# The first modulation of a macaron block: two of eight slices summed by VectorE and ScalarE instead of by small matmuls

## Chip, cores and metric

The kernel runs on one core of a Trainium2 chip, as one program in one launch. The metric is the device time of an execution in microseconds. The profile comes from one execution that the hardware profiler recorded; its engines are called PE (TensorE's matmuls), PEld (TensorE's weight loads), DVE (VectorE), ACT (ScalarE), POOL (GpSimd) and SP (SyncE, which issues the transfers).

## What is computed

One residual block over 512 tokens of width 1024, in float32: a SwiGLU feed-forward half step, a token mixer (gated DeltaNet heads beside latent attention) and a second feed-forward half step. Each of the three reads its input through an adaptive norm, whose shift, scale and gate come from a linear map of a conditioning vector:

```
sc = silu(c)                                  # c: (1, 1024)
mod = sc @ w_ada + b_ada                      # w_ada: (1024, 9 * 1024)
sh1, s1, g1, sh2, s2, g2, sh3, s3, g3 = split(mod, 9)
h = rms(x) * (1 + s1) + sh1                   # x: (512, 1024)
x = x + 0.5 * g1 * swiglu(h, ffn1_w_in, ffn1_w_out)   # d_ff = 2816
x = x + g2 * mixer(rms(x) * (1 + s2) + sh2)
x = x + 0.5 * g3 * swiglu(rms(x) * (1 + s3) + sh3, ffn2_w_in, ffn2_w_out)
```

The change concerns the first modulation alone, that is `sh1` and `s1`: 2 x 1024 numbers, each a sum over the 1024 entries of `sc`.

## The kernel before

The state is kept transposed: eight tiles `xT[kt]` of 128 features x 512 tokens. Every product is made in three passes, since both factors are split into a high part in fp32r and a low remainder (`hh`, `hl` for the activations, `wh`, `wl` for the weights); `mm3` (lines 445 to 449) is one such product of a 128x128 tile of weights with 512 columns.

`phase0` is the first stage. It transposes x, takes the norm, makes the first modulation, and already computes the first six tiles of the feed-forward's first product (three of the gate, three of the other half) into six banks of accumulators `pu`. It goes over the eight slices `kt` of 128 features. For each slice three things are loaded by `phase0_load` (512 KB, 512 KB and 384 KB): the 1024 x 128 pieces of `w_ada` for the shift and for the scale into one tile `ar` of 128 x 8 x 2 x 128 (three buffers), and the 128 x 768 weights of the six tiles into `wr` (four buffers). Loads of two slices are issued ahead of the loop, and step kt issues that of slice kt + 2.

The sum over the 1024 entries of `sc` has eight parts of 128. `phase0_cols` (line 589) makes it on TensorE: for each part the column of `sc`, spread to 32 columns, is the stationary side and 256 columns of `ar` are streamed; the parts go two by two to four groups of 32 columns of the array, so that four partial sums stand in four groups of partitions of an accumulator `pg`. Line 596 is that matmul (sixteen instructions a slice in the trace), and line 599 copies the result to `sg` on ScalarE. `columns` (line 512) then turns the row into two columns with two matmuls: `sg` is stationary, and `sel4`, a column with a one in each of the four groups, adds the four partial sums (line 515). VectorE adds the bias (lines 516 and 517).

In step kt of the loop, the modulation of slice kt + 1 is made while slice kt is multiplied: at the head of the step the sixteen matmuls of slice kt + 1 and (from kt = 1 on) the split of its weights, `wh` on ScalarE (line 217) and `wl` on VectorE (line 218); after two of the six tiles the columns, and then `modulate`: `hm` on VectorE (line 639), `hh` on ScalarE (line 641), `hl` on VectorE (line 633). In step 0 the order of products is another one (lines 555, 571, 572), and the split of slice 1's weights comes behind its modulation.

The whole stage is written inside `in_order` (line 143): its instructions stay in the written order on each engine, SyncE's queue too. Outside such blocks a planner decides, when the program is built, where an instruction goes on its engine; it may put an instruction without such an order between two that have one. Behind the stage, `ada_rest` (line 736) sums the rest of the modulation on VectorE in a like manner (lines 762 and 764, a scaled addition over 512 columns), from tiles that take the memory that `ar` leaves, and `plain` goes on with the feed-forward's other tiles.

Of the kernel before, what the change touches and what calls it, by code (L numbers as in the profile page):

```python
# [15 lines left out]
AF = mybir.ActivationFunctionType  # L16
ALU = mybir.AluOpType
AX = mybir.AxisListType

P = 128  # L20
NT = 512
D = 1024
KT = D // P
# [4 lines left out]
HALF = NT // 2  # L28
KPARTS = ((0, 8), (8, 8), (16, 6))
SEVEN = range(9, 19), range(5, 19)  # L30


def drain(*gens):
# [56 lines left out]
class Block:  # L90
# [51 lines left out]
    @contextmanager  # L142
    def in_order(self, ends=None):

        with self.traced() as block:
            yield
        self.ends = dict(ends or {})
        for i in block:
            if i.engine in self.ends:
                self.follow(i, self.ends[i.engine])  # L150
            self.ends[i.engine] = i.name
# [249 lines left out]
    def plan_units(self):  # L401
# [14 lines left out]

        ffn(ins["ffn1_w_in"][0], ins["ffn1_w_out"][0], 3, range(KT), SEVEN[0])
        w = ins["w_in"][0]
# [58 lines left out]
    def phase0(self):  # L477

        nc = self.nc
        xall = self.const([P, KT, NT], s="xT")  # L480
        self.xT = [xall[:, t, :] for t in range(KT)]
        ss = self.const([P, 2 * NB], s="ss")
        loads = [self.phase0_load(0), self.phase0_load(1)]
        pv = self.aux()
        nc.tensor.transpose(pv[:, :80], self.vecs[:80, :], self.ident[:80, :80])
        self.sc = self.const([P, 8], s="sc")
        nc.scalar.activation(self.sc, pv[:, 72:80], AF.Silu)
        self.vT = self.const([P, 72], s="vT")
        nc.vector.tensor_copy(self.vT, pv[:, :72])
        self.sel4 = self.const([P, 1], s="sel4")  # L490
        nc.vector.tensor_reduce(out=self.sel4, in_=self.ident[:, 0:P:32], axis=AX.X, op=ALU.add)

        def raw(b, j):
            pt = self.aux()
            for t in range(4):
                nc.tensor.transpose(pt[:, t * P:(t + 1) * P], self.xtok[b][j][:, t * P:(t + 1) * P], self.ident)
            nc.vector.tensor_copy(xall[:, 4 * j:4 * j + 4, b * P:(b + 1) * P], pt.rearrange("p (t c) -> p t c", t=4))

        tiles = [(b, j) for b in range(NB) for j in range(2)]
        for b, j in tiles:  # L500
            nc.scalar.activation(self.slot(s="jk"), self.xtok[b][j], AF.Square, accum_out=ss[:, 2 * b + j:2 * b + j + 1])
        for i in (2, 0, 1, 3):
            raw(*tiles[i])
        v = self.small(NB, "v")
        nc.vector.tensor_reduce(out=v, in_=ss.rearrange("p (b j) -> p b j", j=2), axis=AX.X, op=ALU.add)
        r = self.rms_cols(v, NB, D)
        for i in (4, 5, 6):
            raw(*tiles[i])
        self.c1, self.c2 = self.const([P, KT], s="sh"), self.const([P, KT], s="s1")
        self.new_h()  # L510

        def columns(kt, sg, pg):
            k = slice(kt, kt + 1)
            for m in range(2):
                nc.tensor.matmul(pg[:, 256 + m:257 + m], sg[:, m * P:m * P + P], self.sel4, start=True, stop=True)
            nc.vector.tensor_tensor(out=self.c1[:, k], in0=pg[:, 256:257], in1=self.vT[:, k], op=ALU.add)
            nc.vector.scalar_tensor_tensor(out=self.c2[:, k], in0=pg[:, 257:258], scalar=1.0, in1=self.vT[:, 8 + kt:9 + kt],
                                           op0=ALU.add, op1=ALU.add)

        def weights(kt):  # L520
            raw, hi, lo = loads[kt][1]
            self.split_w(raw[:, :6, :], hi[:, :6, :], lo[:, :6, :])
            return hi, lo


        xn = self.slot(s="xn")
        for b in range(NB):
            nc.vector.tensor_scalar(out=xn[:, b * P:(b + 1) * P], in0=self.xtok[b][0][:, :P], scalar1=r[:, b:b + 1],
                                    scalar2=None, op0=ALU.mult)
        dg = self.diag(r)  # L530
        cols = self.phase0_cols(0, loads[0][0])
        raw0, wh, wl = (x[:, :6, :] for x in loads[0][1])
        w = wh, wl
        nc.scalar.copy(wh, raw0)
        pt = self.aux()
        for b in range(NB):
            nc.tensor.transpose(pt[:, b * P:(b + 1) * P], xn[:, b * P:(b + 1) * P], self.ident)
        t, m = self.slot(s="hm"), self.slot(s="hm")
        nc.vector.tensor_copy(t, pt)
        columns(0, *cols)  # L540
        hh, hl = self.h[0]
        nc.scalar.activation(hh, t, AF.Identity, scale=self.c2[:, 0:1], bias=self.c1[:, 0:1])
        nc.vector.tensor_scalar(out=m, in0=t, scalar1=self.c2[:, 0:1], scalar2=self.c1[:, 0:1], op0=ALU.mult, op1=ALU.add)
        nc.vector.tensor_tensor(out=hl, in0=m, in1=hh.bitcast(F32), op=ALU.subtract)
        nc.vector.tensor_tensor(out=wl, in0=raw0, in1=wh.bitcast(F32), op=ALU.subtract)
        raw(*tiles[7])
        pu = [self.acc() for _ in range(3)] + [self.aux() for _ in range(3)]
        for kt in range(KT):
            (hi, lo), (xh, xl) = w, self.h[kt]
            more = kt + 1 < KT  # L550
            if kt + 2 < KT:
                loads.append(self.phase0_load(kt + 2))
            if kt == 0:
                for j in range(6):
                    nc.tensor.matmul(pu[j], hi[:, j, :], xh, start=True, stop=False)
                rb = self.slot(s="rb")
                nc.scalar.copy(rb, self.spread_diag(dg, NB))
            for j in range(6):
                if j == 0 and more:
                    cols = self.phase0_cols(kt + 1, loads[kt + 1][0])  # L560
                    if kt > 0:
                        w = weights(kt + 1)
                if j == 2 and more:
                    columns(kt + 1, *cols)
                    self.modulate([kt + 1], slice(0, NT), rb, self.c2, self.c1)
                    if kt == 0:
                        w = weights(kt + 1)
                if kt > 0:
                    self.mm3(pu[j], hi[:, j, :], lo[:, j, :], xh, xl, False, kt == KT - 1)
                else:  # L570
                    nc.tensor.matmul(pu[j], hi[:, j, :], xl, start=False, stop=False)
                    nc.tensor.matmul(pu[j], lo[:, j, :], xh, start=False, stop=False)
        return pu
# [15 lines left out]
    def phase0_cols(self, kt, a):  # L589

        nc = self.nc
        pg = self.aux()
        for q in range(4):
            for e in range(2):
                kc = 2 * q + e
                nc.tensor.matmul(pg[32 * q:32 * q + 32, :256], self.sc[:, kc:kc + 1].to_broadcast([P, 32]),  # L596
                                 a[:, kc], start=(e == 0), stop=(e == 1), tile_position=(0, 32 * q))
        sg = self.slot(s="sg")[:, :256]
        nc.scalar.copy(sg, pg[:, :256])
        return sg, pg  # L600


    def new_h(self):
# [1510 lines left out]
```

## Time and profile before

| what | us |
|---|---|
| median of 3 runs | 1058.62 (1057.68 to 1059.16) |
| profiled execution, its own time | 1057.94 |
| its span, first to last instruction | 1056.2 |
| busy: PE / PEld / DVE / ACT / POOL | 1035.7 / 904.3 / 722.5 / 471.2 / 25.2 |
| mean granted clock of TensorE | 0.997 |

Times in the profile are counted from the start of the span. A matmul's recorded end is modelled, and consecutive matmuls overlap in the records; the chain of work that ended last gives each the time that it adds. A row of the timeline has the start, the duration, the engine, the line, the operation with its output and inputs, the count, and in brackets the idle time of the engine before it and what ended that. A row of the groups has line, engine, operation, names and shapes, the count, then busy us and the mean ns of one. A row of the waits has who waited for whom, the sum of us, how often, and the longest.

### The profile page before, as it was taken

How to read it: one execution, taken by the hardware profiler on the slowest of the kernel's cores; microseconds unless marked ns; L12 is line 12 of the kernel's file. 1: busy time of each engine (PE TensorE's matmuls, PEld its weight loads, DVE VectorE, ACT ScalarE, POOL GpSimd, SP SyncE). 2: the span in 40 equal slices, each digit the busy share in tenths (PEclk: the TensorE clock that was granted, in tenths of full speed). 3: DMA queues.
4: the chain of work that ended last, by engine and by line, in shares of the span. 5: the costliest groups of instructions: out<-in, count | busy, mean ns of one | idle time of the engine just before them, and what ended most of it. 6: DMA issues, size and time to landing. Idle time of an engine off the chain costs nothing.

```text
span 1056.2 us, 16319 instructions
## 1 busy us (share of the span) xinstructions
PE 1035.7 (98%) x6417; PEld 904.3 (86%) x6417; DVE 722.5 (68%) x1280; ACT 471.2 (45%) x857; POOL 25.2 (2%) x74
## 2 busy tenths in 40 slices
PE   6999999999999999999999989999999999999998
PEld 5788799998887798888788769998999999778887
DVE  4479978769888547558787477788688886842221
ACT  3342345555222225469864554354455556422221
POOL 0000000000100000100000001100000000000000
PEclk8999999999999999999999999999999999999999
DMA  9988234343789435211232021113333344723320
GB/s 276 285 260 278 82 100 119 102 121 91 256 287 339 130 96 158 78 40 41 61 80 66 21 80 41 40 42 99 98 103 101 102 119 141 227 76 111 112 62 30
DMA packets 208028, 130.74 MB, mean 124 GB/s; under 512 B 13890, under 2 KB 192079, under 8 KB 207951
## 3 DMA queue, kind: packets, MB, share of 16 engines
q1 hardware_dynamic: 207950, 129.69, 41.3%
q8 instruction: 50, 0.82, 0.3%
q14 instruction: 28, 0.22, 0.1%
HBM read 127.18 MB, written 2.49 MB: 123 GB/s over the span
## 4 chain that ended last, share of the span: by engine, by line
PE 89%; DVE 5%; ACT 2%; DMA 2%; issue 2%; SPq 0%; POOL 0%; DVEq 0%; POOLq 0%; ACTq 0%
PE pa L447 18%; PE pa L448 18%; PE pa L449 18%; PE pa L335 13%; PE pb L335 10%; PE pb L447 1%; PE pb L448 1%; PE pb L449 1%; PE pb L596 1%; PE pb L1847 1%; DVE wl L218 1%; PE pb L1827 1%; DMA xt<-in_x 0%; DVE cv L1391 0%; ACT bd L1477 0%
## 5 line engine op out<-in xcount | busy, mean ns | idle before, releaser
L217 ACT CAST wh<-wr 128x1024 fp32r<-128x1024 f32 (+1 forms) x116 | 116.4, 1008 | 245.8 <-PE pa L448 216.7
L218 DVE TENSOR_TENSOR wl<-wr,wh 128x1024 fp32r<-128x1024 f32 (+1 forms) x116 | 135.3, 1169 | 117.5 <-ACT wh L217 113.3
L447 PE MATMUL pa<-hh,wh 128*128 128x512 f32 (+1 forms) x453 | 174.8, 386 | 1.6 <-ACT sg L808 1.6
L448 PE MATMUL pa<-hl,wh 128*128 128x512 f32 (+1 forms) x453 | 172.8, 381 | 0.0
L449 PE MATMUL pa<-hh,wl 128*128 128x512 f32 (+1 forms) x453 | 172.7, 381 | 0.0
L447 PE MATMUL pa<-ah,wh 128*128 128x512 f32 (+1 forms) x396 | 146.6, 370 | 0.0
L449 PE MATMUL pa<-ah,wl 128*128 128x512 f32 (+1 forms) x396 | 144.9, 366 | 0.0
L448 PE MATMUL pa<-al,wh 128*128 128x512 f32 (+1 forms) x396 | 144.8, 366 | 0.0
L447 PEld LDWEIGHTS pa<-hh,wh 128*128 128x128 f32 x453 | 85.3, 188 | 20.7 <-ACT sg L808 3.0
L449 PEld LDWEIGHTS pa<-hh,wl 128*128 128x128 f32 x453 | 85.3, 188 | 15.8 <-DVE wl L218 0.4
L448 PEld LDWEIGHTS pa<-hl,wh 128*128 128x128 f32 x453 | 85.4, 188 | 14.3 <-DVE hl L633 0.2
L447 PEld LDWEIGHTS pa<-ah,wh 128*128 128x128 f32 x396 | 74.7, 189 | 14.3 <-ACT wh L217 1.7
L449 PEld LDWEIGHTS pa<-ah,wl 128*128 128x128 f32 x396 | 74.7, 189 | 12.3
L448 PEld LDWEIGHTS pa<-al,wh 128*128 128x128 f32 x396 | 74.7, 189 | 11.8
L764 DVE SCALAR_TENSOR_TENSOR aa<-ar,sc,aa 128x512 f32<-128x512 f32 x98 | 73.0, 749 | 9.3 <-DMA ar<-in_w_ada 7.7
L252 DVE TENSOR_TENSOR wl<-sf,wh 128x1024 fp32r<-128x1024 f32 x48 | 58.6, 1222 | 30.0 <-ACT wh L256 30.0
L335 PE MATMUL pa<-hh,wh 128*128 128x256 f32 x192 | 54.5, 284 | 0.0
L335 PE MATMUL pa<-th,wh 128*128 128x256 f32 x192 | 54.3, 283 | 0.0
L335 PE MATMUL pa<-tl,wh 128*128 128x256 f32 x192 | 54.3, 283 | 0.0
L335 PE MATMUL pa<-th,wl 128*128 128x256 f32 x192 | 54.3, 283 | 0.0
L335 PE MATMUL pa<-hl,wh 128*128 128x256 f32 x192 | 54.3, 283 | 0.0
L335 PE MATMUL pa<-hh,wl 128*128 128x256 f32 x192 | 54.3, 283 | 0.0
(434 smaller groups left out, 2214.1 us busy)
## 6 DMA issues: line engine op xcount, KB each, us to landing
wr<-in_ffn_w_in SPq DMA_DIRECT2D x79, 512.0 KB, 3.8
ar<-in_w_ada SPq DMA_DIRECT2D x80, 256.0 KB, 5.9
ar<-in_w_ada SPq DMA_DIRECT2D x32, 512.0 KB, 7.6
wr<-in_ffn_w_out SPq DMA_DIRECT2D x32, 512.0 KB, 3.9
wr<-in_w_in SPq DMA_DIRECT2D x21, 512.0 KB, 3.7
wr<-in_ffn_w_out SPq DMA_DIRECT2D x16, 384.0 KB, 3.6
wr<-in_w_out SPq DMA_DIRECT2D x8, 512.0 KB
wr<-in_ffn_w_in SPq DMA_DIRECT2D x8, 384.0 KB, 7.0
```

Of the source, the lines that this page charges most:

```text
L217: self.nc.scalar.copy(hi, raw)
L218: self.nc.vector.tensor_tensor(out=lo, in0=raw, in1=hi.bitcast(F32), op=ALU.subtract)
L252: sub = lambda out, x, y: nc.vector.tensor_tensor(out=out, in0=x, in1=y, op=ALU.subtract)
L335: nc.tensor.matmul(z, a[:, j, :], b, start=start and j == 0 and i == 0, stop=j == 3 and i == 2, skip_group_check=not start)
L447: mm(out, wh, xh, start=start, stop=False)
L448: mm(out, wh, xl, start=False, stop=False)
L449: mm(out, wl, xh, start=False, stop=stop)
L596: nc.tensor.matmul(pg[32 * q:32 * q + 32, :256], self.sc[:, kc:kc + 1].to_broadcast([P, 32]), a[:, kc], start=(e == 0), stop=(e == 1), til ...
L764: nc.vector.scalar_tensor_tensor(out=acc, in0=a, scalar=sc, in1=acc, op0=ALU.mult, op1=ALU.add)
L1827: nc.tensor.matmul(ps[:, :n], self.qnT[h][:, ts], self.knT[h][:, :n], start=True, stop=False)
L1847: nc.tensor.matmul(po[:, :P], pT[:, b * P:(b + 1) * P], v[b][:, h * P:(h + 1) * P], start=(b == 0), stop=(b == i))
```

## The change

Slices 5 and 7 (`SUMMED`) no longer go through the sixteen small matmuls. `phase0_sums` makes their sum per partition: ScalarE multiplies the first of the eight parts by its entry of `sc` (128 x 256), and seven scaled additions of VectorE add the others, each onto the result of the one before. The partition sum that is left is made by the two column matmuls, with a column of ones instead of `sel4`. The sum for slice kt + 2 is written at the head of step kt, and its instructions are left out of the order written by hand (`loose`), so that the planner places them. For these two slices the columns stand at the head of the step before any product; for the others they now stand after one tile instead of two. The loads of three slices are issued ahead of the loop, and step kt issues that of slice kt + 3.

```diff
+SUMMED = (5, 7)
 ...
     def in_order(self, ends=None):
+        self.loose = set()
         with self.traced() as block:
             yield
         self.ends = dict(ends or {})
         for i in block:
+            if i.name in self.loose:
+                continue
             if i.engine in self.ends:
                 self.follow(i, self.ends[i.engine])
             self.ends[i.engine] = i.name
 ...
-        loads = [self.phase0_load(0), self.phase0_load(1)]
+        loads = [self.phase0_load(kt) for kt in range(3)]
 ...
-        def columns(kt, sg, pg):
+        def columns(kt, sg, pg, ones):
             k = slice(kt, kt + 1)
             for m in range(2):
-                nc.tensor.matmul(pg[:, 256 + m:257 + m], sg[:, m * P:m * P + P], self.sel4, start=True, stop=True)
+                nc.tensor.matmul(pg[:, 256 + m:257 + m], sg[:, m * P:m * P + P], ones, start=True, stop=True)
 ...
+        sums = {}
         for kt in range(KT):
             (hi, lo), (xh, xl) = w, self.h[kt]
             more = kt + 1 < KT
-            if kt + 2 < KT:
-                loads.append(self.phase0_load(kt + 2))
+            if kt + 3 < KT:
+                loads.append(self.phase0_load(kt + 3))
 ...
             for j in range(6):
+                if j == 0 and kt + 2 in SUMMED:
+                    sums[kt + 2] = self.phase0_sums(loads[kt + 2][0])
                 if j == 0 and more:
-                    cols = self.phase0_cols(kt + 1, loads[kt + 1][0])
+                    if kt + 1 in SUMMED:
+                        cols = sums[kt + 1], self.aux(), self.ones[:, 0:1]
+                    else:
+                        cols = self.phase0_cols(kt + 1, loads[kt + 1][0])
                     if kt > 0:
                         w = weights(kt + 1)
-                if j == 2 and more:
+                if j == (kt + 1 not in SUMMED) and more:
                     columns(kt + 1, *cols)
 ...
-        return sg, pg
+        return sg, pg, self.sel4
+
+    def phase0_sums(self, a):
+        nc = self.nc
+        sg = self.slot(s="sg")[:, :256]
+        with self.traced() as block:
+            nc.scalar.activation(sg, a[:, 0], AF.Copy, scale=self.sc[:, 0:1])
+            for kc in range(1, KT):
+                nc.vector.scalar_tensor_tensor(out=sg, in0=a[:, kc], scalar=self.sc[:, kc:kc + 1], in1=sg, op0=ALU.mult,
+                                               op1=ALU.add)
+        self.loose.update(i.name for i in block)
+        return sg
```

## The prediction

> **What bounds the kernel now.** I read the page first, then the chain that ended last, cut to the stage that the change touches, then the timeline of VectorE and ScalarE there, and last the transfers.
>
> ```profile
> PE 1035.7 (98%) x6417; PEld 904.3 (86%) x6417; DVE 722.5 (68%) x1280; ACT 471.2 (45%) x857; POOL 25.2 (2%) x74
> 33.23:39.02 5.79, 5.79 (x40) 4.23 (x39) 2.59 (x5) 1.83 (x3) 0.00 (x0) 1.00 1.11 305
> 39.02:44.80 5.78, 5.78 (x40) 4.22 (x39) 2.60 (x5) 1.83 (x3) 0.00 (x0) 1.00 1.14 310
> 50.58:56.36 5.78, 5.78 (x40) 4.22 (x39) 2.63 (x6) 1.83 (x3) 0.00 (x0) 1.00 0.46 122
> ```
>
> The first row is the busy time by engine. The others are the windows of slices kt=2, 3 and 5: length, then busy us of PE, PEld, DVE, ACT and POOL, PE clock, DMA share, GB/s. TensorE is busy for the whole 5.78 us of a slice at full clock; VectorE works 2.6 us of it and ScalarE 1.8. So what leaves TensorE leaves the time, as long as nothing that TensorE needs comes later. The chain shows of what a slice is made (start, us, what); kt=3 first, then the head of kt=1:
>
> ```profile
> 39.09 1.02 PE pb L596 x16
> 40.11 0.43 PE pa L447
> 40.53 0.23 PE pa L448
> ...
> 41.69 0.34 PE pb L515 x4
> 42.03 0.34 PE pa L447
> ...
> 44.87 1.02 PE pb L596 x16
> ```
>
> ```profile
> 28.66 0.23 PE pa L448
> 28.90 0.50 PE pa L449
> 29.40 0.23 PE pa L447
> PEld pa L449 <- DVE wl L218: 0.4, 1, 0.4
> ```
>
> A slice opens with the sixteen small matmuls of L596 that make the next slice's modulation (1.02 us), and the first product behind them takes 0.43 instead of 0.23. The columns (L515) take 0.34 after two tiles, and the product behind those 0.34. In kt=1 one product waits for the low half of its weights: 0.50 where its neighbours take 0.23 or 0.24.
>
> **The change part by part.** The sum is made against the profiled execution (1057.94 us, span 1056.2); the median of the runs shown, 1058.62, lies 0.68 above it, and I take the difference to the median.
>
> *Removed from TensorE.* In the two slices that open with L596 for slices 5 and 7 (kt=4 and kt=6) the sixteen matmuls go: 1.02 + (0.43 - 0.23) = 1.22 us each, on the path, 2.44 in all. The two column products stay; with a column of ones in place of the selector they have the same shape. The eviction of L599 goes from ScalarE too.
>
> *Columns one tile earlier.* This takes nothing off TensorE, but the modulation starts 3 x 0.23 = 0.69 us sooner (two products sooner in kt=0). The 0.26 us of kt=1 goes with it: wl of slice 1 is queued behind that modulation, so it comes 0.46 earlier. What is late next is the eviction: `sg` ends 40.20 + 0.37 = 40.57 (rows below), and the columns now start near 40.11 + 0.43 + 2 x 0.23 = 41.0 with their weight load 0.2 before. That fits by 0.2; I take 0, and 0.1 a slice, 0.5 in all, if it fails.
>
> *Added to VectorE and ScalarE.* The rows of kt=3, in whose slice the sum for slice 5 is written:
>
> ```profile
> 38.23 0.75 DVE L633 SCALAR_TENSOR_TENSOR hl<-hm,sh,hh 128x512 fp32r<-128x512 f32 x1 [0.79 <-ACT hh L641]
> ...
> 40.20 0.37 ACT L599 COPY sg<-pb 128x256 f32<-128x256 f32 x1 [2.00 <-PE pb L596]
> ...
> 41.34 0.96 DVE L218 TENSOR_TENSOR wl<-wr,wh 128x768 fp32r<-128x768 f32 x1 [2.36 <-ACT wh L217]
> ...
> 42.22 0.15 DVE L516 TENSOR_TENSOR sh<-pb,vT 128x1 f32<-128x1 f32 x1
> ...
> 42.47 0.75 DVE L639 SCALAR_TENSOR_TENSOR hm<-xT,s,rb 128x512 f32<-128x512 f32 x1
> ...
> 43.26 0.73 ACT L641 ACTIVATE hh<-hm,sh 128x512 fp32r<-128x512 f32 x1 [1.95 <-DVE hm L639]
> ...
> 44.02 0.75 DVE L633 SCALAR_TENSOR_TENSOR hl<-hm,sh,hh 128x512 fp32r<-128x512 f32 x1 [0.79 <-ACT hh L641]
> ```
>
> Each summed slice adds one ScalarE pass and seven VectorE additions over 128x256, each reading the one before. The nearest rows:
>
> ```profile
> L665 ACT ACTIVATE sq<-xT 128x256 f32<-128x256 f32 x14 | 5.8, 418 | 8.9 <-DVE xT L2039 8.9
> L639 DVE SCALAR_TENSOR_TENSOR hm<-xT,mod,pb 128x256 f32<-128x256 f32 x32 | 15.0, 476 | 2.7 <-PE pb L619 2.7
> 701.10 0.48 DVE L639 SCALAR_TENSOR_TENSOR hm<-xT,mod,pb 128x256 f32<-128x256 f32 x1
> 701.49 0.48 DVE L633 SCALAR_TENSOR_TENSOR hl<-hm,mod,hh 128x256 fp32r<-128x256 f32 x1
> 81.64 3.10 DVE L764 SCALAR_TENSOR_TENSOR aa<-ar,sc,aa 128x512 f32<-128x512 f32 x4
> ```
>
> Additions that don't need each other start 0.39 us apart. The chain of four in the last row is the same operation on 512 columns, each reading the last: (3.10 - 0.75) / 3 = 0.78 apart; 0.75 - 0.476 = 0.27 less for 256 columns gives 0.51. Seven make 3.55 us (2.75 if 0.39 held), plus 0.42 on ScalarE ahead of them. I take the chain's spacing, as its row is the same operation in the same dependence. The Trainium skill says otherwise (VectorE: DVE Perf Modes, The DRAIN you can't avoid): chaining without semaphores gains nothing, so a dependence costs nothing extra; by it the sum would be the 2.75, and the stall below 0.8 smaller. The trace speaks against it with 0.78 for a dependent chain.
>
> When can they start? The sum needs both halves of its slice's modulation weights.
>
> ```profile
> 24.77 2.11 SPq L128 DMA_DIRECT2D ar<-in_w_ada  x2
> 30.54 2.01 SPq L128 DMA_DIRECT2D ar<-in_w_ada  x2
> 40.20 1.72 SPq L128 DMA_DIRECT2D ar<-in_w_ada  x2
> ar<-in_w_ada SPq DMA_DIRECT2D x1, 512.0 KB, 7.6
> ```
>
> These are slices 4, 5 and 7 at SyncE's queue; the last row is the landing time of the transfer issued at 24.77: it lands at 32.4. Up to the second half of slice 5 follow 512 + 384 + 1024 KB, 1.97 MB, at the 305 to 310 GB/s of the windows 6.4 us: slice 5 is there at 38.8 (37.5 to 39.5 as bounds, since the rate is a mean). Loading three slices ahead doesn't move that: SyncE issues the loads in the same order, nothing else stands between them, the stream runs at a DMA share of 1.1, and a load still waits for the buffer of the slice three before. I cost that edit at 0; if it does bring slice 5 in sooner, that is the first rival below.
>
> So the seven additions run 39.3 to 42.85, with the pass on ScalarE, which idles then, ahead of them. The column products of slice 5 now stand at the head of kt=4, at 44.87 - 0.26 = 44.6: the sum itself is in time. But VectorE also owes slice 4 its wl, columns, hm and hl. With the sum first, by the distances in the rows above, wl starts at 42.85, hm 1.13 later, hh ends 0.79 + 0.73 after that at 45.5 and hl 0.78 later at 46.3. TensorE wants hh at 44.6 + 0.34 = 44.95 and hl one product later: 0.55 + 0.4, about 1.0 us of stall. With the sum threaded into VectorE's waits (0.8 us for hh in each slice) all of it ends near 45.3 and the stall is 0.4. I take 0.7.
>
> Slice 7: issued at 40.20, both halves there at 48.2 by the stream's rate, 49.5 by 7.6 us from its second half, some 1.7 after the first. Its sum is wanted at the head of kt=6, near 55.6 (56.36 less 0.26 and 1.22, plus 0.7). From 49.5 on it runs 50.0 to 53.5; wl, columns, hm and hh of slice 6 follow by the distances above to 56.15, where TensorE wants hh at 55.95: 0.2 of stall, 0.5 with hl. From 48.2 on there is none. The stream's rate is what the loads before it go by, so I take 0 and keep 0.5.
>
> *Moved behind.* SyncE's next loads wait for the last reader of these buffers.
>
> ```profile
> SPq L128 <- PE pb L596: 3.6, 2, 3.2
> 57.54 1.41 SPq L128 DMA_DIRECT2D ar<-in_w_ada  x3
> ```
>
> They waited 3.2 us for L596 of slice 7; now for its sum, near 53.5. In that stretch the DMA share is 0.46, so they and the weights queued behind them come some 4 us sooner. TensorE waits for none of them before, so I count 0.
>
> Sum: -2.44 - 0.26 + 0.7 = -2.0 us, 1056.6. Alone this case reaches from -2.3 (a stall of 0.4) to -0.7 (stalls of 1.0 and 0.5, and 0.5 for the eviction), 1056.3 to 1057.9.
>
> **The rivals.**
>
> *All of it hides.* If slice 5 lands 1 us sooner, or the chain runs at 0.39, the stall goes: -2.7, 1055.9. For it: the loads are written earlier. Against it: a stream that is already full, and the spacing of L764.
>
> *The sums stand in the queues before their data.* The sums are kept out of the handwritten order, so a planner places them where it believes data and engine are ready. How it does with such instructions shows elsewhere:
>
> ```profile
> 53.91 0.16 DVE L1322 COPY ex<-vb 128x4 f32<-128x4 f32 x1
> DVE aa L764 <- DMA ar<-in_w_ada: 2.2, 2, 1.9
> DVE aa L762 <- DMA ar<-in_w_ada: 1.7, 1, 1.7
> 65.00:75.00 10.00, 10.00 (x46) 8.28 (x45) 9.53 (x13) 3.23 (x5) 0.00 (x0) 1.00 1.04 293
> ```
>
> A free instruction was put between two ordered ones at 53.91, and where transfers are as dense as here (DMA share 1.04) VectorE stood 1.9 and 1.7 us before data that the planner had expected. Had it expected slice 5 over 3.4 us early, four additions would fill VectorE's gap in kt=2 before wl of slice 3 (the 2.36 us that end at 41.34 above, a slice of 5.78 and the 0.26 sooner: up to 35.3), and the pass on ScalarE would stand before a cast. They wait to 39.25 and end at 41.3; wl, columns, hm and hh follow by 0.88 + 0.25 + 0.79 + 0.73, to 43.95, where TensorE wanted hh at 40.11 - 0.26 = 39.85: 4.1 us of stall. Then -2.7 + 4.1 = +1.4, up to +2.7 if slice 7 does the same for the 1.3 us between its two landing times; middle +2.1, 1060.7, slower. An error of under 3.4 us puts at most one addition before hl of slice 3, which has that much room. For it: the two waits. Against it: they are half of 3.4. The Trainium skill states the ground of this rival (Perfetto Trace Analysis, Per-engine timelines): VectorE and ScalarE are strict FIFO, so nothing passes a waiting instruction; the two waits above agree, as VectorE idled in them with the weights of that stage queued behind.
>
> *The later stages give it back.* The mixer's order is made anew by the same planner, and TensorE has waits there:
>
> ```profile
> PE pb L1599 <- DVE vb L1179: 2.0, 2, 1.6
> ```
>
> One more wait like its longest costs 1.6 us: -0.4, 1058.2, no change that can be measured; one less would give -3.6.
>
> **How the numbers follow.** About 0.2% (2.1 us) is what a measurement of this kernel can tell from no change; the lines are 1056.5 and 1060.7. Forecast 0.46, of it 0.22 faster and 0.24 same, since 1056.6 lies on the first line and more of its own range above it; all hidden 0.20, faster; queues 0.28, of it 0.20 slower and 0.08 same, since most of 1060.0 to 1061.3 lies above the second line; later stages 0.06, same. That makes 0.42 faster, 0.38 same and 0.20 slower. The range reaches from 1055.4 (all hidden, with 0.5 of the waits in the later stages gone too) to 1060.7, the middle of the queue rival; outside it lie half of that rival and a little of the hidden case, under 2 in 10.
>
> **What would show it.** Right: L596 with six times sixteen matmuls instead of eight, none in kt=4 and kt=6; 7 x 2 new VectorE additions near 0.48 us, 0.51 apart; a PE wait for hh or hl (L641, L633) of 0.4 to 1.0 us about 45 us; kt=6 without one; the 0.50 at L449 gone; and the products of kt=6 beginning near 55.6 + 0.34. Wrong: the ScalarE pass or the first addition standing before a cast or hm with a DMA as its releaser before 38 us; a PE wait at L515 in every slice; slice 5's loads landing before 37 us; or a stage shorter by 2 us with a total that isn't, which would put the cause behind it.

## The result, and the profile after

The changed kernel took 1054.97 us (median of 6 runs, 1054.27 to 1055.53), the kernel before in the same comparison 1058.29 (1057.10 to 1059.88): a ratio of 0.9968, 95% interval 0.9955 to 0.998. That is 3.3 us faster; 2.0 were forecast, and the time lies 0.4 below the range. The profiled execution took 1054.27 us, its span is 1052.6, 3.6 below that of before.

What was to go is gone. From the groups of the changed kernel: six times sixteen small matmuls instead of eight, and fourteen additions.

```profile
L606 PE MATMUL pb<-ar,sc 128*32 128x256 f32 x96 | 6.5, 385 | 2.8 <-DMA ar<-in_w_ada 2.8
L619 DVE SCALAR_TENSOR_TENSOR sg<-ar,sc,sg 128x256 f32<-128x256 f32 x14 | 6.8, 483 | 3.0 <-ACT sg L617 2.7
```

But the loop did not become 2.0 us shorter. Two marks show it: the sixteen matmuls that make slice 1's modulation, and the last product of slice 7. In the timeline of TensorE before, and then of after (start, duration, what; L447 to L449, L515, L596 and L599 are L451 to L453, L519, L606 and L609 in the changed kernel):

```profile
22.70 1.09 PE L596 MATMUL pb<-ar,sc 128*32 128x256 f32 x16
...
65.91 0.39 PE L449 MATMUL pb<-hh,wl 128*128 128x512 f32 x1
```

```profile
20.17 1.09 PE L606 MATMUL pb<-ar,sc 128*32 128x256 f32 x16
...
39.28 0.61 PE L519 MATMUL pb<-sel,sg 128*128 128x1 f32 x4 [0.96 <-ACT sg L609]
...
44.05 0.58 PE L519 MATMUL pb<-ones,sg 128*128 128x1 f32 x4 [0.61 <-DVE sg L619]
...
45.10 0.50 PE L452 MATMUL pa<-hl,wh 128*128 128x512 f32 x1
...
63.30 0.39 PE L453 MATMUL pb<-hh,wl 128*128 128x512 f32 x1
```

Before, the stretch between the marks is 65.91 - 22.70 = 43.21 us; after, 63.30 - 20.17 = 43.13. The stage ends 2.61 earlier because it *starts* 2.53 earlier, which no part of the change was meant to do. The windows from 15 to 22 us of before and of after (length, then busy us of PE, PEld, DVE, ACT, POOL, TensorE's granted clock, DMA share, GB/s) say why:

```profile
15.00:22.00 7.00, 6.72 (x31) 4.88 (x24) 3.88 (x9) 1.92 (x3) 0.00 (x0) 0.53 1.15 303
```

```profile
15.00:22.00 7.00, 6.25 (x48) 3.71 (x41) 3.59 (x8) 2.88 (x5) 0.00 (x0) 1.00 1.15 303
```

In the execution before, TensorE ran its first products at half clock, after not. I call these a late and an early start. In the loop itself the matmuls saved are eaten by waits. Three windows of after, each 5.78 us long as a slice was before. The first ends at the columns of slice 4 (39.28, in kt=3), the second holds those of slice 5 (44.05, the head of kt=4), the third those of slice 7 (54.90, the head of kt=6):

```profile
33.50:39.28 5.78, 4.82 (x32) 3.02 (x30) 2.22 (x6) 1.54 (x4) 0.00 (x0) 1.00 1.14 306
39.28:45.06 5.78, 5.07 (x24) 3.82 (x24) 5.28 (x13) 2.13 (x3) 0.00 (x0) 1.00 1.14 305
50.50:56.28 5.78, 5.78 (x31) 4.88 (x30) 4.89 (x12) 2.42 (x4) 0.00 (x0) 1.00 0.55 163
```

TensorE, full in the windows of slices 2, 3 and 5 before, lacks 0.96 and 0.71 us in the first two and nothing in the third. The chain that ended last, cut to 36 to 62 us (start, us, what), holds what it waits for:

```profile
30.58 7.78 DMA ar<-in_w_ada
38.47 0.52 ACT sg L617
39.01 0.50 DVE sg L619
...
40.97 0.95 DVE wl L222
...
42.85 0.67 DVE hm L661
43.54 0.73 ACT hh L663
44.30 0.76 DVE hl L655
45.10 0.50 PE pa L452
```

Before, this stretch of the chain held TensorE alone. Now it begins with a transfer: slice 5's modulation weights land at 38.4, the sum starts, VectorE owes slice 4 its `wl`, `hm` and `hl` as well, and the product at 45.10 waits for `hl`. From 45.10 on TensorE needs 18.2 us to the last mark and waits for nothing more.

ScalarE shows how the pass stands in its queue (timeline, in brackets the idle time before and its releaser):

```profile
38.47 0.51 ACT L617 ACTIVATE sg<-ar,sc 128x256 f32<-128x256 f32 x1 [2.98 <-DMA ar<-in_w_ada]
38.88 0.35 ACT L609 COPY sg<-pb 128x256 f32<-128x256 f32 x1
```

The planner put it ahead of the copy of slice 4's own sums. That copy's matmuls were done near 37.4 (36.33 + 1.09), but it waited with the pass until 38.88; this is TensorE's 0.96 us at 39.28.

The rest of the 3.6 us lies far behind, in the mixer. The waits of TensorE from 530 to 565 us before (who for whom, sum, times, longest; after there are none), and SyncE's queue there before and then after:

```profile
PE pb L1528 <- DVE t L1179: 1.1, 1, 1.1
```

```profile
552.48 1.14 SPq L1501 DMA_DIRECT2D t_d<-bt  x2
...
556.84 0.37 SPq L1503 DMA_DIRECT2D t<-t_d  x1
```

```profile
549.87 1.13 SPq L1523 DMA_DIRECT2D t_d<-bt  x2
...
552.55 0.37 SPq L1525 DMA_DIRECT2D t<-t_d  x1
```

A block is written to DRAM (`t_d`) and read back. From the issue of the write to that of the read it took 4.36 us before and 2.68 after, the read landing 2.9 and 3.5 later: 1.1 us less in all, and the wait of 1.1 is gone. So the span's -3.6 is -2.6 by the first stage's end, -1.1 here, and 0.1 given back elsewhere.

### The profile page after: what moved, and what is told of

It reads as the page before. It is cut to its first block, busy times and chain, and to the rows that moved or that the text cites. A ratio compares the mean times of both kernels' runs of the same rounds, so it can differ in the third digit from the quotient of the medians.

```text
span 1052.6 us, 16272 instructions
## 1 busy us (share of the span) xinstructions
PE 1030.1 (98%) x6385; PEld 900.6 (86%) x6385; DVE 728.4 (69%) x1294; ACT 470.9 (45%) x857; POOL 25.2 (2%) x74
## 3 DMA queue, kind: packets, MB, share of 16 engines
HBM read 127.18 MB, written 2.49 MB: 123 GB/s over the span
## 4 chain that ended last, share of the span: by engine, by line
PE 86%; DVE 6%; ACT 3%; DMA 2%; issue 2%; SPq 1%; POOL 0%; ACTq 0%; DVEq 0%; POOLq 0%
PE pa L451 18%; PE pa L452 18%; PE pa L453 17%; PE pa L339 13%; PE pb L339 10%; DMA ar<-in_w_ada 2%; PE pb L1869 1%; DVE wl L222 1%; DVE cv L1413 1%; PE pb L451 1%; PE pb L452 1%; PE pb L453 1%; PE pb L1849 1%; SPq L129 1%; ACT bd L1499 0%
## 5 line engine op out<-in xcount | busy, mean ns | idle before, releaser
L451 PE MATMUL pa<-hh,wh 128*128 128x512 f32 (+1 forms) x453 | 174.8, 386 | 1.6 <-ACT sg L830 1.6
L453 PE MATMUL pa<-hh,wl 128*128 128x512 f32 (+1 forms) x453 | 172.8, 381 | 0.0
L451 PE MATMUL pa<-ah,wh 128*128 128x512 f32 (+1 forms) x396 | 146.7, 371 | 0.0
L453 PE MATMUL pa<-ah,wl 128*128 128x512 f32 (+1 forms) x396 | 145.1, 366 | 0.0
L451 PEld LDWEIGHTS pa<-hh,wh 128*128 128x128 f32 x453 | 85.4, 188 | 19.9 <-ACT sg L830 3.0
L453 PEld LDWEIGHTS pa<-hh,wl 128*128 128x128 f32 x453 | 85.3, 188 | 15.3
L451 PEld LDWEIGHTS pa<-ah,wh 128*128 128x128 f32 x396 | 74.7, 189 | 14.3 <-ACT wh L221 1.7
L453 PEld LDWEIGHTS pa<-ah,wl 128*128 128x128 f32 x396 | 74.7, 189 | 12.2
```

The lines of the kernel that those rows point to most:

```text
L451: mm(out, wh, xh, start=start, stop=False)
L453: mm(out, wl, xh, start=False, stop=stop)
```

## The experiments

Theory 1: TensorE's start varies from execution to execution; the changed stage ends at what slice 5's landing allows, so it gains when the start is late and nothing when it is early. Theory 2: the change itself brings the early start. Theory 3: the mixer's wait went because the planner, which orders everything anew, gave it another order.

**The kernels again.** The same code as before and after, timed 12 times each on another chip.

> The kernel before, unchanged, for its start: in the profile of before the first small matmuls of slice 1 began at 22.77 us, with TensorE's clock granted at 0.5 from 15.4 to 22.2; in the profile of after they began at 20.24 at full clock. Theory 1 (chance of the start, and slice 5's landing near 38.5 us takes an early start back in the changed kernel only): either start may show here, and the first products of the tiles behind the stage begin 43.5 us after the first small matmuls of slice 1 whichever it is, so the span moves with the start, 1053.7 for an early one and 1056.2 for a late one. Theory 2 (the change itself brings the clock sooner): a late start, 22.5 to 23, in every profile of this kernel. On the wait of 1.1 us for VectorE at L1528 in the mixer: theory 3 (the planner's order differs) has it here too, a chance of the run may not.

> The changed kernel, unchanged, for its start. Theory 1: if the start is late (slice 1's small matmuls near 22.7), the waits of 1.0 to 1.4 us at the columns of slice 4 (L519) and behind slice 5's columns shrink to under 0.5 in all and the stage ends at the same 63.7 us within 0.5; if it is early they are there again, 2.6 us in all. Theory 2: an early start again (20.2). Theory 3: no wait at L1550.

Measured: 1056.71 (ratio 0.9997, 0.9986 to 1.0009) and 1055.69 (0.9983, 0.9973 to 0.9994). The profiled execution of the kernel before started early here, so theory 2 isn't needed for an early start. It lost 1.3 us of it again (20.09 to 64.63, 44.54 between the marks). A row of VectorE's timeline, and the waits of TensorE from 23 to 62 us:

```profile
53.87 0.17 DVE L1322 COPY ex<-vb 128x4 f32<-128x4 f32 x1 [2.47 <-DMA vb<-in_gdn_a_log]
```

```profile
PE pa L447 <- ACT hh L641: 0.6, 1, 0.6
PE pa L448 <- DVE hl L633: 0.3, 1, 0.3
```

A four-column copy, put by the planner in front of slice 6's `hm`, waited 2.47 us for a small transfer. With a late start that transfer is there in time. The mixer's wait was there again (1.0). The changed kernel started early, and waited more than in its first profile (44.63 between the marks): 1.4 and 0.6 us for the sums, and 0.7 for slice 6's `hh` and `hl`, behind the same copy `ex`. The gain of the first comparison shrank too, from 3.3 us to 1.4: the 35 runs of the kernel before that were timed beside these go down to 1055.55 (median 1057.05), while the six of the first comparison had none below 1057.10.

**Parts of the change.** The earlier columns and loads alone; and the sums in the order written by hand.

```diff
-SUMMED = (5, 7)
+SUMMED = ()
```

> No slice is summed by VectorE; columns after one tile and loads three ahead stay. By the steps of the prediction -0.26 us (the wait for wl of slice 1 gone) and nothing else in the first stage: ratio 0.9997, eight groups of sixteen small matmuls, no wait at L519. Theory 2 in the form that the written order brings the clock sooner: the start early as in after and -2.5 us. Theory 3 in the form that the columns alone make the planner's order differ: no wait at L1528's place and -1.1 more.

```diff
-                if j == 0 and kt + 2 in SUMMED:
-                    sums[kt + 2] = self.phase0_sums(loads[kt + 2][0])
 ...
-                if j == (kt + 1 not in SUMMED) and more:
+                if j == (3 if kt + 1 in SUMMED else 1) and more:
+                    adds = iter(())
+                    if kt + 2 in SUMMED:
+                        sums[kt + 2], adds = self.phase0_sums(loads[kt + 2][0])
                     columns(kt + 1, *cols)
-                    self.modulate([kt + 1], slice(0, NT), rb, self.c2, self.c1)
+                    steps = self.modulated([kt + 1], slice(0, NT), rb, self.c2, self.c1)
+                    next(steps)
+                    for _ in range(2):
+                        next(adds, None)
+                    drain(steps)
+                    drain(adds)
```

> The sums of slices 5 and 7 stand in the written order: ScalarE's pass behind the cast of the next slice's weights, two additions in VectorE's wait for hh and five behind hl, and the columns of the summed slices after three tiles. If the stall of 2.6 us comes from where the planner put the pass (in front of the copy of slice 4's sums, L609) and from columns at the head of a step, it goes: from slice 1's small matmuls to the first products of the next tiles 43.5 - 2.7 = 40.8 us, at most 0.5 more, and with an early start 2.5 us less time than after. If slice 5's landing itself holds TensorE wherever the sum stands, the wait moves to the columns of slice 5 and the time is that of after.

Measured: 1056.78 (0.9989, 0.9977 to 1.0) and 1057.67 (1.0001, 0.999 to 1.0011). The columns alone, with a late start, take 22.68 to 65.84, 43.16: the wait of 0.26 for `wl` is gone, and all but 0.05 of it is lost elsewhere, some 0.1 in kt=0, where the weight load of the columns waits 0.3 for the eviction. The sums in the written order have a median 2.0 us above that of the changed kernel, where the planner puts them. Their profile doesn't show why: it is of the fastest of the twelve runs (1055.68), its stage is as long as that of the changed kernel here (44.41 between the marks against 44.63), and it waits for slice 6's `hh` behind the copy `ex` too.

**Starting TensorE by hand, first try.** Eight transposes fill its gap at 12 us; 21 more push the first product back.

```diff
         dg = self.diag(r)
+        pd = self.aux()
+        for _ in range(8):
+            nc.tensor.transpose(pd[:, :P], self.ident, self.ident)
 ...
         pu = [self.acc() for _ in range(3)] + [self.aux() for _ in range(3)]
+        for _ in range(21):
+            nc.tensor.transpose(pu[0][:, :P], self.ident, self.ident)
```

> The kernel before with eight extra transposes of the identity (output not read) in the 12 to 14.3 us gap of TensorE, so that its clock should stay up from then on. Theory 1 (start and landing): the start is early in every run, span near 1054.3 in all of them, time near 1056.0, no run near 1058; the spread of the kernel before (1055.5 to 1060.6) shrinks to under 1 us. Rival (the changed kernel's gain does not hang on the start): the spread stays, median 1057.

> The changed kernel with the same eight transposes. Theory 1: the early start costs it its stalls again, so it stands only 0.3 to 0.8 us below the kernel before with the same transposes, near 1055.4; additions of slice 5 wait for a landing at 38.5 and TensorE for them by 0.9 to 1.6 us in the heads of kt=3 and kt=4. Rival (the gain does not hang on the start): it stands 1.6 to 2.7 us below that kernel.

> The kernel before with the eight transposes, and with 21 more of them directly ahead of the first product, which push TensorE's first products back by about 2.5 us at full clock: a late start by hand. Both theories: 2.3 to 2.7 us above the same kernel without the 21, near 1058.5, since TensorE is full from there on.

> The changed kernel with the eight and the 21 transposes. Theory 1: the 2.5 us are hidden, as slice 5 lands at 38.5 whatever TensorE does: 0 to 0.5 us above the changed kernel without the 21, near 1055.7, some 2.8 below the kernel before with the 21 (ratio 0.9973); TensorE's waits in kt=3 and kt=4 for the sums shrink from over 2 us to under 0.6. Rival (the gain does not hang on the start): 2.3 to 2.7 us above the changed kernel without the 21, and as far below the kernel before as the two without the 21 are apart.

Measured: 1055.85 (0.9986, 0.9976 to 0.9997), 1057.51 (1.0002, 0.9992 to 1.0012), 1056.59 (0.9993, 0.9985 to 1.0001) and 1057.84 (1.0011, 0.9999 to 1.0023). All four profiles have a clock of 1.00 from 15 to 22 us, and the first median is near the 1056.0 expected, but its runs still spread to 1059.0: in the profiled one TensorE waited 1.8 us for slice 6's `hh`, behind the copy `ex`, and its clock was 0.79 from 55 to 63 us. The totals of the changed kernels fit neither theory: they are slower than without the transposes. The profile puts that in the mixer. Waits of TensorE from 530 to 565 us of the changed kernel with the eight:

```profile
PE pb L1872 <- ACT pT L1868: 1.2, 1, 1.2
PE pb L1553 <- DVE t L1204: 0.8, 1, 0.8
```

The kernels before with the same transposes have none there. In the first stage the changed pair answers as theory 1 has it: the start is 1.14 later (20.52 and 21.66), the end is not (65.00 and 64.76). But the 21 moved the start by half of what was meant, and the copy `ex` disturbed three of the four, so this was done again below.

**Taking single waits away.** The copy `ex` ordered behind the stage, in the kernel before and in the changed one; with that, the pass of the sums behind the cast of the next weights; and slice 7 alone summed.

```diff
             with self.in_order():
                 pu = self.phase0()
+            self.p0_end = self.ends[mybir.EngineType.DVE]
 ...
-        v.tensor_copy(ea, self.alog)
+        self.follow(v.tensor_copy(ea, self.alog).ins, self.p0_end)
```

> The kernel before with one small VectorE copy (ex<-vb, L1322, which waits for a small late transfer) ordered behind the first stage's modulation work instead of where the planner put it, in front of slice 6's hm. Theory 1 (the stage ends at the later of two bounds, TensorE's start and what VectorE waits for): with an early start TensorE's waits for hh and hl at 48 to 52 us (0.9 us in the repeat, 2.1 with the eight transposes) go, and the first stage ends 2.5 us before that of the profiled execution of the kernel before instead of 1.3 before; with a late start nothing changes. Median 0.3 to 0.8 us below the kernel before. Rival (the run-to-run spread of the stage does not come from such waits): ratio 1.000, waits still there behind another instruction.

> The changed kernel with the same copy ordered behind. Theory 1: the copy's wait stands behind those for slice 5's sums, so 0.3 us at most against the changed kernel, near 1055.4; TensorE's waits for sg of L609 and L619 (1.0 to 1.5 and 0.6 us with an early start) stay. Rival (the copy is what holds the changed kernel back too): 1.0 us or more below 1055.7.

```diff
-                if j == 0 and kt + 2 in SUMMED:
-                    sums[kt + 2] = self.phase0_sums(loads[kt + 2][0])
 ...
                     if kt > 0:
                         w = weights(kt + 1)
+                    if kt + 2 in SUMMED:
+                        sums[kt + 2] = self.phase0_sums(loads[kt + 2][0])
 ...
+        nc.scalar.activation(sg, a[:, 0], AF.Copy, scale=self.sc[:, 0:1])
         with self.traced() as block:
-            nc.scalar.activation(sg, a[:, 0], AF.Copy, scale=self.sc[:, 0:1])
```

> The changed kernel with the copy ordered behind and the sum's ScalarE pass in the written order, behind the cast of the next slice's weights, so that it cannot stand in front of slice 4's copy. Theory 1: the wait of L519 for sg of L609 (1.0 to 1.5 us) goes; what is left with an early start is what VectorE owes late after slice 5 landed at 38.5, 0.5 to 1.2 us; first stage 1.0 to 1.5 us shorter than the changed kernel's with an early start, same with a late one, median 1054.2 to 1055.2 against 1055.7. Rival (the data itself is the floor, not the queue in front of it): no shorter than the changed kernel, the wait only moves to L519 for sg of L619.

```diff
-SUMMED = (5, 7)
+SUMMED = (7,)
```

> The changed kernel with slice 7 alone summed; slice 5 takes its sixteen matmuls again. Leaves nothing out. Theory 1: no wait in kt=3 and kt=4; a late start gives the kernel before less 1.22 and 0.26 = 1.5 us, an early one the same less the 1.3 us that it loses at kt=6: median about 1.3 us below the kernel before, ratio 0.9988, and 0 to 1 us above the changed kernel, since slice 5's sum saves 1.2 with a late start and loses 1.4 with an early one. Rival (both slices save alike): 1.2 us slower than the changed kernel in every start.

Measured: 1057.06 (1.0002, 0.9993 to 1.0011), 1055.16 (0.9981, 0.9973 to 0.999), 1063.31 (1.0057, 1.0039 to 1.0075) and 1057.83 (1.0006, 0.9993 to 1.0018).

The first's profiled execution had a late start, in which the copy costs nothing, so it told nothing on the copy, and the median (1057.06 against 1057.12) doesn't show the 0.3 to 0.8 us expected. The kernel below with the copy behind and an early start by hand has no such wait. The third was to be the fastest and is the slowest. With the pass no longer in front, the planner spread the additions between slice 4's `wl`, `hm` and `hl`, the last two behind slice 5's `wl`, and did the same at slice 7, so both sums came late: the wait only moved to L519 for `sg` of L619, as the rival had it. TensorE's timeline, and two windows, the first behind the first wait, the second from within the second wait on:

```profile
45.31 0.58 PE L519 MATMUL pb<-ones,sg 128*128 128x1 f32 x4 [2.91 <-DVE sg L619]
...
60.34 1.01 PE L519 MATMUL pb<-ones,sg 128*128 128x1 f32 x4 [2.85 <-DVE sg L619]
```

```profile
47.50:52.00 4.50, 4.50 (x22) 3.27 (x24) 0.75 (x1) 0.20 (x1) 0.00 (x0) 0.73 0.98 265
58.00:66.00 8.00, 5.66 (x15) 4.65 (x16) 5.93 (x12) 2.60 (x4) 0.00 (x0) 0.64 0.67 220
```

A wait of 2.9 us is followed by a clock of 0.73 and 0.64, so it costs about twice: the marks are 51.68 us apart (20.33 to 72.01), 8.4 more than with the copy behind alone (43.26), for 4.4 us more of such waits.

Slice 7 alone has no wait in kt=3 and kt=4 and takes 42.25 us between the marks (20.52 to 62.77), 0.96 less than before; two waits of 1.2 us each in the mixer hide it in the profiled total. The median was expected 1.3 us below the kernel before and is 0.7 above, and 2.1 above the changed kernel (1055.69, on another chip), where 0 to 1 was expected. Four of its twelve runs have a mean clock of 0.995 and a span of 1057.5 or more; none of these was profiled, so where their time goes is open.

The runs of the second are a sign of theory 1 that needs no hand. Each run has a span and a mean clock; one late start alone makes the mean 0.997, as in the profile before. The reverse does not hold: the kernel before with eight transposes has 0.997 with an early start, its clock having fallen behind a wait. Of the kernel before, timed beside these four, the eight runs at 0.997 have a median span of 1055.9 and the eleven at 1.0 one of 1054.3. Of the changed kernel with the copy behind, those at 0.996 and 0.997 have 1053.0 to 1054.0, the three at 0.998 1053.0 to 1054.2, those at 1.0 1053.4 to 1053.5: its time does not depend on the clock.

**Three more profiles**, one execution each: the changed kernel twice, the kernel before once.

> The changed kernel, one more profiled execution. Theory 1 (VectorE owes slice 4's weights, hm and hl and slice 5's seven additions after the landing at 38.5, done near 45, whatever TensorE does): if TensorE starts late (first products of kt=1 near 27.7, clock at half speed before), its waits in kt=3 and kt=4 sum to 0.4 to 1.0 us and the first stage ends near 63.2 to 63.8, 2.0 us or so before that of the kernel before with a late start; if it starts early, they sum to 2.2 to 2.8 and the stage ends at 62.8 to 64.5. Rival (the waits belong to the change, not to the start): 2.2 us or more in either start. Wait for t in the mixer: if it belongs to the compiled program, no wait of TensorE at L1550 above 0.3 us, as in its two earlier profiles; if to the run, about 1.1 in some.

> The same as for the look before it: with a late start waits of 0.4 to 1.0 us in kt=3 and kt=4, with an early one 2.2 to 2.8; no wait at L1550 if the mixer's wait belongs to the program.

> The kernel before, one more profiled execution. If the mixer's wait for t belongs to the compiled program: 1.0 to 1.1 us at L1528 again, as in its two earlier profiles. If it belongs to the run: 0 or 1.1. First stage: no wait with a late start, end near 65.4; with an early one the wait for hh behind the copy ex (0.9 to 2.1 us), end near 64.2.

Measured: 1055.32, 1056.1 and 1057.4. Both profiles of the changed kernel had an early start (43.60 and 44.42 between the marks), that of the kernel before a late one, so the late start of the changed kernel stayed unseen. Its waits in kt=3 and kt=4 were 1.5 us in both, less than the 2.2 to 2.8 expected; 0.3 and 0.9 more came at slice 6. TensorE's waits from 530 to 565 us are 0.4, 0.2 and 0.5.

**Starting TensorE by hand, again**, the copy `ex` behind the stage in all, the transposes written into tiles that are there anyway, and 29 ahead of the first product.

```diff
     def phase0_cols(self, kt, a):
 ...
         pg = self.aux()
+        for _ in range(8 * (kt == 0)):
+            nc.tensor.transpose(pg[:, :P], self.ident, self.ident)
 ...
+        for _ in range(29):
+            nc.tensor.transpose(pu[0][:, :P], self.ident, self.ident)
```

> The kernel before with the copy ordered behind the stage and eight transposes written into slice 0's own tile, so that the start is early. Theory 1: no wait of TensorE in the first stage, which ends near 63.0, 2.4 before the kernel before with a late start and level with the changed kernel with the copy behind (63.3). Rival (the waits belong to the change, not to the start): 63.0 too, but then the late pair below differs by no more than this one.

> The same with 29 more transposes ahead of the first product, so that TensorE starts about 2.3 us later at full clock. Both theories: no wait in the stage, which ends near 65.3; time 2.0 to 2.6 us above the same kernel without the 29.

> The changed kernel with the copy behind, the eight and the 29 transposes. Theory 1 (VectorE is done near 45 whatever TensorE does): waits of 0.3 to 1.0 us in kt=3 and kt=4 instead of 2.2 to 2.8, stage end 63.2 to 63.8, so the 2.3 us of later start cost 0 to 0.5, and the stage is 1.5 to 2.1 us shorter than the kernel before with the same start, against 0 with the early one. Rival (the waits belong to the change, not to the start): waits of 2.2 us or more again, stage end near 65.5, level with the kernel before with the late start.

Measured: 1054.87 (0.9974, 0.9962 to 0.9985), 1057.24 (0.9997, 0.9988 to 1.0007) and 1055.60 (0.9983, 0.9972 to 0.9994). The marks of the three, in this order, in TensorE's timelines:

```profile
20.38 1.09 PE L598 MATMUL pb<-ar,sc 128*32 128x256 f32 x16
...
63.59 0.39 PE L449 MATMUL pb<-hh,wl 128*128 128x512 f32 x1
```

```profile
22.37 1.09 PE L600 MATMUL pb<-ar,sc 128*32 128x256 f32 x16
...
65.58 0.39 PE L449 MATMUL pb<-hh,wl 128*128 128x512 f32 x1
```

```profile
22.91 1.09 PE L610 MATMUL pb<-ar,sc 128*32 128x256 f32 x16
...
63.83 0.39 PE L453 MATMUL pb<-hh,wl 128*128 128x512 f32 x1
```

With the changed kernel with the copy behind (20.46 to 63.72; it started early by itself, without transposes) this is a two by two:

| | early start | late start by hand |
|---|---|---|
| kernel before: from mark to mark / end of stage | 43.21 / 63.59 | 43.21 / 65.58 |
| changed kernel: the same | 43.26 / 63.72 | 40.92 / 63.83 |

The kernel before pays a late start in full (1.99 us). The changed one pays 0.11 for 2.45: slice 4's `hl` begins at 44.39 with the early start and at 44.77 with the late one, so VectorE's side hardly moves. The medians agree: the 29 transposes cost the kernel before 2.4 us (1054.87 to 1057.24), and the changed kernel with the late start lies 0.4 above that with the early one (1055.60 and 1055.16, on two chips, with ratios of 0.9983 and 0.9981). The chain from 36 to 62 us, summed by line, first with the early and then with the late start, shows what bounds it:

```profile
by line: DMA ar<-in_w_ada 29.3%; PE pa L452 12.7%; PE pa L451 11.4%; PE pa L453 10.6%; DVE sg L619 8.9%; PE pb L451 7.9%; PE pb L453 7.9%; PE pb L452 7.8%; PE pb L606 3.9%; DVE wl L222 3.7%; DVE hl L655 2.9%; ACT hh L663 2.8%; PE pb L519 2.
```

```profile
by line: PE pa L451 17.4%; PE pa L452 15.7%; PE pa L453 15.2%; PE pb L451 13.2%; PE pb L453 13.2%; PE pb L452 13.1%; PE pb L610 7.8%; PE pb L519 5.2%
```

Early, the transfer, VectorE and ScalarE carry it up to 45 us; late, TensorE alone, and the waits for sums are gone. What is left with the late start is a product that takes 0.40 instead of 0.23, since its weight load waits for `hl` (a piece of the chain, and a row of the waits):

```profile
45.68 0.40 PE pa L452
PEld pa L452 <- DVE hl L659: 0.2, 1, 0.2
```

The rival, that the waits belong to the change, had 65.5 for the end; it falls.

The kernel before with an early start and no sums at all is as fast as the changed kernel: a ratio of 0.9974 to the kernel before, on the chip where the changed kernel with its late start has 0.9983. An early start together with slice 7's sum alone was not run.

## Why the prediction was wrong, point by point

The sum was made against one execution with a late start, as if the start were the same in all. In the profiled pair its terms read: the start, which had no term, -2.53 us; the matmuls and the earlier columns -2.44 - 0.05 = -2.49; the stall 43.13 - 40.72 = +2.41, where +0.7 was said; the later stages -1.1, where 0 was said; and +0.1 elsewhere, together -3.6. So the step that failed is the stall, with the fixed start under it, and the 0 for the later stages left out another 1.1 us of gain. That -2.0 still lies near -2.6, the first stage's part, is luck: the start's -2.5 and the 1.7 by which the stall was too small largely cancel. Point by point:

- **Sixteen matmuls gone, -2.44:** right as work. With a late start by hand the loop is 43.21 - 40.92 = 2.29 shorter; with an early one 0.05 longer.
- **The wait for `wl` in kt=1, -0.26, and the eviction, 0 (0.5 if it fails):** the wait went as said, but the columns alone save 0.05, so some 0.2 is lost again. About 0.1 of it is the eviction's doubt come true in kt=0; where the rest is lost isn't shown. Together the two terms are near 0.
- **The stall, +0.7 (0.4 to 1.0; 1.5 with slice 7's):** this step failed. Its mechanism is the one in the chain, and its times were near: landing 38.4 where 38.8 was said, the additions (3.08 - 0.48) / 5 = 0.52 apart where 0.51 was, slice 7's sum without a wait. By what the prediction draws from the Trainium skill (VectorE: DVE Perf Modes, The DRAIN you can't avoid), whose measurement is of copies with and without semaphores, the spacing would have been 0.39; the trace bears out the chain. What failed is that TensorE's side of the race was taken from one profiled execution with a late start. With a late start the stall is 0.2 (2.49 expected from the two points above, 2.29 measured); with an early one it is 2.5, where 40.72 us (43.21 - 2.49) would be the loop without a stall and 43.26 was measured. The prediction's bounds held neither.
- **The sums in the queue before their data (the slower rival):** half right in place, not in price. ScalarE idled 2.98 us before the pass, with slice 4's copy and cast queued behind it, and TensorE waited 0.96 for the copy, far from the 4.1 us priced: the pass stood in kt=3 before slice 4's copy and cast, not in kt=2 before slice 3's cast. The Trainium skill (Perfetto Trace Analysis, Per-engine timelines) calls ScalarE strict FIFO, so that nothing passes a waiting instruction; the trace agrees, as the copy's input was ready near 37.4 and it ran at 38.88.
- **Loads three ahead, 0:** right; slice 5 lands with the stream. **Moved behind:** the next loads' issue at 57.54 is now at 52.98 (53.5 was said), and no wait depends on it.
- **Later stages, 0 (rival: one wait less, 1.6):** wrong by 1.1 in the profiled pair. The rival's -3.6 for one wait less meets the measured pair's only by luck, since the first stage's terms under it were others. And it was not the planner's order, so theory 3 falls: the two programs have the same order on VectorE through the mixer (from 450 to 620 us on TensorE, ScalarE and SyncE's queue too), and the kernel before with transposes, in that order too, shows no wait there in four profiles. The kernel before itself shows 0.5 to 1.2 in three, the changed one 0 to 0.4 in four, its variants up to 2.6. How long the block takes through DRAM differs between programs and somewhat between executions; why is open.

What the change is worth thus hangs on the start: with a late one by hand in both kernels the loop is 2.3 us shorter and the median 1.6 lower (1055.60 against 1057.24), with an early one in both the loop is as long. The measured -3.3 of the medians also holds which starts the runs happened to have (it was -1.4 in the repeat) and the mixer's wait. How much of it each makes isn't shown. Nor is theory 2 wholly out: of the kernels without transposes, all eight profiles with sums had an early start and one of five without. If the change favours the early start, it gains nothing by it, since its stage then ends where a late start would end it (63.72 and 63.83).

## What to carry to other kernels

Before an engine is relieved, ask what else could end the stage just behind it: here a transfer that lands at 38.4, with 6.7 us of ScalarE's and VectorE's work behind it, cost TensorE 0.2 us in an execution with a late start and 2.5 in one with an early start. Take the start of the stage from several executions, not from one, and read the granted clock in its first windows; eight throwaway transposes in the gap, with one small copy moved, gave this kernel as much as the whole change. And leave a queue's head to what is ready: moving one pass behind a cast, to spare a wait of 1 us, cost 8.

## What the runs showed of the hardware

TensorE's clock in the first 22 us differs between executions of the same kernel, 0.53 or 1.00 from 15 to 22 us, worth 2.5 us at the first mark; with 1.04 us of transposes in its gap it was 1.00 in all seven profiles. Before that stretch TensorE stands idle for 2 to 3 us (in brackets below), first in before, where the clock fell to half speed, then in after, where it did not:

```profile
14.47 1.17 PE L596 MATMUL pb<-ar,sc 128*32 128x256 f32 x16 [2.00 <-DVE xn L528]
```

```profile
14.26 1.09 PE L606 MATMUL pb<-ar,sc 128*32 128x256 f32 x16 [2.81 <-DMA ar<-in_w_ada]
```

So the length of the gap alone does not decide it. Later in the stage a wait of 1.77 us was followed by half clock (the kernel before with eight transposes), and waits of 1.37 and 1.47 us in the changed kernel, without and with the transposes, were not. The Trainium skill (TensorE: Matmul & The Clock Gate, What's actually happening) says that the gate watches free-running windows of 3.4 us, so that the moment of transition depends on where the first work lies in them; the variation agrees with it, though no run here shows where the windows lie.

A pass of ScalarE over 128x256 with a scale per partition takes 0.51 us, where the row of a square of that size had 0.42.
